# A norm factor by one moving column, a spread in two halves, a fifth filler tile, and the residual update's order pinned anew

## The chip, the cores and the metric

The kernel runs on one core of one Trainium2 chip, as one program. The metric is the time on the device, in microseconds (us), as the median of several executions; the profile is one more execution of the same program, taken by the hardware profiler. A core has five engines with an instruction queue each, worked off in order: TensorE (PE, with its weight loads as PEld), VectorE (DVE), ScalarE (ACT), GpSimd (POOL) and SyncE (SP, which here only issues DMAs). They meet through semaphores: an instruction waits until another engine's count has reached a value.

## The reference, cut to what matters

Two layers over 256 tokens of width 2048. Layer 0 mixes tokens with a state-space mixer, layer 1 with an attention; both layers end in the same tail:

```python
h = x
for i in range(DEPTH):
    hn = rmsnorm(h, norm_mix_pre[i])
    mix = ssd_mixer(hn, ...) if i % 2 == 0 else fox_mixer(hn, ...)
    h = h + rmsnorm(mix, norm_mix_post[i])
    ff = swiglu(rmsnorm(h, norm_ffn_pre[i]), ffn_w_gate[i], ffn_w_up[i], ffn_w_down[i])
    h = h + rmsnorm(ff, norm_ffn_post[i])
    pe = rmsnorm(p[i] @ ple_w_proj[i], ple_norm[i])
    h = h + sigmoid(h @ ple_w_gate[i]) * pe
```

The two lines that add a normed branch to `h` are what the change is about: there are two of them in a layer, four in the program. `rmsnorm(y, w)` multiplies each token's row by one factor, 1/sqrt(mean(y*y) + eps), and each column by `w`.

## The kernel before, in words

**Layout.** Activations lie transposed: 16 chunks of 128 model columns (partitions) by 256 tokens. `h[c]` is chunk c of the residual stream, `m[c]` chunk c of a mixer's or feed-forward's output, `xs[c]` the matmul operand made from `h[c]`.

**Matmuls in two parts.** Every large product is formed from float32 numbers split into a high part and a rest. An operand `xs[c]` holds both (`x[:, 0]` high, `x[:, 1]` low, side by side). A weight stage, 128 x 768 or 128 x 1024 numbers, arrives by DMA as `raw`; ScalarE casts it to the high part `wh` (line 176), VectorE subtracts to get the rest `wl` (line 181). A step of a unit is then, for each output tile, `wh` against both halves of the operand (512 columns, line 238) and `wl` against the high half (256 columns, line 240). `emit_stage` issues the DMA, the cast and the subtraction of the next stage, in that order of the weights, and pins where they stand among the other instructions of ScalarE and VectorE (`issue_after`); four buffers of `wh` and `wl` and six of `raw` rotate. A scheduler makes the queues from this; what is pinned stays so.

**Units.** `unit` works through one block of output columns: it takes the stages one after the other (`next_stage`), calls `pre` for the operands that the next steps need, issues the matmuls of the step, and evacuates the accumulators at the end. The first unit behind each of the four norms has six output tiles and 16 steps, with one stage of 128 x 768 and one operand chunk in each step; it can only run as fast as the operands `xs[c]` are made.

**The norm factor** (`post_norm`, line 399). When the last `m[c]` is squared and summed into `ssb` (128 x 256), `rstd_small` (line 293) multiplies it by a 128 x 128 matrix of ones, for the two halves of the tokens, so that each token's sum stands 128 times in PSUM; one column of each half goes through `ms` (line 300) and GpSimd's power (line 303) to `rs`. `rstd_wide` (line 306) puts `rs` on two diagonals `dg` (line 309), and one matmul of 256 columns with the ones spreads the factors over all partitions (line 312); ScalarE copies them to SBUF as `rwide` (line 313). `rstd_small` and `rstd_wide` are used 18 times in the program; only 4 times by `post_norm`, elsewhere in the midst of a unit.

**Fillers.** TensorE would have nothing to do in that time. Eight tiles of the per-layer product `p @ ple_w_proj` (`filler`, 6 matmuls each, lines 390 to 394) are kept for it: two go ahead of `rstd_small`, two (up to `FILL_B`) between it and the spread, four behind the spread. Each tile's result is copied out of PSUM by ScalarE (line 396, `pp`). One weight stage is emitted ahead of the spread and one behind it (`PRE_A`, `PRE_B`).

**The update** (`mk_update`, line 417). For chunk c: VectorE forms `m[c] * w * rwide` (`scaled`, line 430), adds it to `h[c]` (line 436), ScalarE makes the high part of `xs[c]` (line 269, or 266 in the second norm of a layer, where there is no column factor), VectorE the low part (line 270, or 267). VectorE's steps are chained to each other. Before, the row of them for one chunk was: add of c, `scaled` of c+1, low part of c; the stage's `wl` was pinned ahead of the low part, and its cast behind the high part of the same chunk. For the first two chunks a stage is emitted in the update itself, from then on by `next_stage` in each step.

Of the kernel before, what the change touches and what calls it, by code (L numbers as in the profile page):

```python
# [7 lines left out]
F32 = mybir.dt.float32  # L8
# [6 lines left out]
P = 128  # L15
# [19 lines left out]
FILL_B = 4  # L35
PRE_A = 1
PRE_B = 1
TAIL_STAGES = 2
PACED = 2
WARM = 10  # L40
# [15 lines left out]
def tile_trunk(ctx, tc, a, out):  # L56
# [236 lines left out]
    def rstd_small(acc, n):  # L293
        ps = misc()
        for j in range(2):
            PE.matmul(ps[:, j * P:(j + 1) * P], lhsT=acc[:, j * P:(j + 1) * P], rhs=ones,  # L296
                      start=True, stop=True)
        ms = tmp("ms", (P, 2))
        for j in range(2):
            dmark[0] = V.tensor_scalar(out=ms[:, j:j + 1], in0=ps[:, j * P:j * P + 1], scalar1=1.0 / n,  # L300
                                       scalar2=EPS, op0=mult, op1=add)
        rs = tmp("rs", (P, 2), bufs=3)
        G.tensor_tensor(out=rs, in0=ms, in1=mhalf, op=ALU.pow)  # L303
        return rs

    def rstd_wide(rs, o):
# [5 lines left out]
        PE.matmul(ps[:, :T], lhsT=ones, rhs=dg, start=True, stop=True)  # L312
        A.copy(out=o, in_=ps[:, :T])

# [52 lines left out]
    pts = []  # L367
# [10 lines left out]
    def filler(pp, us):  # L378
        st = [None]

        def tile_(u, t):
# [14 lines left out]
            A.copy(out=pp[4 * u + t], in_=acc[:, :T])  # L396
        return [lambda u=u, t=t: tile_(u, t) for u in us for t in range(4)]

    def post_norm(fill):
# [7 lines left out]
        rstd_wide(rs, rwide)  # L407
        for _ in range(PRE_B):
            emit_stage(mark[0], dmark[0])
        for f in fill[FILL_B:]:  # L410
            f()

# [4 lines left out]
    def mk_update(new, m, wpost, wpre, xs):  # L417
# [10 lines left out]
        def scaled(c):  # L428
            ts[c] = new()
            return V.scalar_tensor_tensor(out=ts[c], in0=m[c], scalar=col(wpost, c), in1=rwide,  # L430
                                          op0=mult, op1=mult)

        def up(c):
            if c == 0:
                chain(lambda: scaled(0))
            chain(lambda: V.tensor_tensor(out=h[c], in0=h[c], in1=ts[c], op=add))
# [41 lines left out]
    def tail(i, mpx, m, pp, mk_next):  # L478
        xs = [newx() for _ in range(NCH)]
        post_norm(filler(pp, (0, 1)))  # L480

        with ExitStack() as st:
# [40 lines left out]
            for half in range(2):  # L523
                acts = [ap_.tile([P, 2, T], F32R, tag="a", name=nm("a")) for _ in range(HALF)]
                c0 = 0
                for n in (GU if half == 0 else GU[::-1]):
                    sgs.clear()
                    up = mk_update(new_sg, m, f"mix_post{i}", f"ffn_pre{i}", xs) if first[0] else None
# [37 lines left out]
        post_norm(filler(pp, (2, 3)))  # L566
# [56 lines left out]
        for u, n in enumerate(OUT0):  # L623
            last = u == len(OUT0) - 1
            up = None
            if u == 0:
                up = mk_update(lambda: pn.tile([P, T], F32, tag="pn", name=nm("pn"), bufs=4), m,
                               f"ffn_post{i}", None, xs2)
# [540 lines left out]
```

## Time and profile before

| | |
|---|---|
| Time before, median of 3 runs | 2781.67 us (2781.13 to 2782.24) |
| The profiled execution's own time | 2781.57 us |
| Its span, first to last instruction | 2779.8 us |
| PE busy | 2758.7 us (99% of the span) |
| DVE busy | 1909.7 us (69%) |
| ACT busy | 1482.3 us (53%) |
| Spread matmuls of the four norms start at | 697.99, 1442.82, 1935.64, 2680.46 us |

Times in rows are counted from the span's start. A row of the timeline gives start, length, engine, line, operation, output<-inputs, shape and count, and in brackets how long the engine had been idle and who ended that. Instructions of one engine overlap a little: the next starts before the last has ended, so the rate is read from the starts. A line of the waits gives who waited for whom, the total, how often, and the longest.

### The profile page before, as it was taken

How to read it: one execution, taken by the hardware profiler on the slowest of the kernel's cores; microseconds unless marked ns; L12 is line 12 of the kernel's file. 1: busy time of each engine (PE TensorE's matmuls, PEld its weight loads, DVE VectorE, ACT ScalarE, POOL GpSimd, SP SyncE). 2: the span in 40 equal slices, each digit the busy share in tenths (PEclk: the TensorE clock that was granted, in tenths of full speed). 3: DMA queues.
4: the chain of work that ended last, by engine and by line, in shares of the span. 5: the costliest groups of instructions: out<-in, count | busy, mean ns of one | idle time of the engine just before them, and what ended most of it. 6: DMA issues, size and time to landing. Idle time of an engine off the chain costs nothing.

```text
span 2779.8 us, 43097 instructions
## 1 busy us (share of the span) xinstructions
PE 2758.7 (99%) x16306; PEld 2446.8 (88%) x16306; DVE 1909.7 (69%) x3165; ACT 1482.3 (53%) x2455; POOL 50.8 (2%) x104
## 2 busy tenths in 40 slices
PE   9999999999999999999999999999999999999999
PEld 8888888889888888888898998888888888888898
DVE  8888888855876645666668656766876545666577
ACT  6586676544654444444446544545554444445454
POOL 0000000000000000000000000000000000000000
PEclk9999999999999999999999999999999999999999
DMA  7666665565666656666556576555666556656554
GB/s 252 198 198 188 190 191 174 156 205 177 184 193 190 191 190 189 189 178 198 193 163 194 168 213 192 178 160 159 195 189 195 191 190 185 193 171 203 196 166 159
DMA packets 262511, 520.08 MB, mean 187 GB/s; under 512 B 17392, under 2 KB 42128, under 8 KB 262304
## 3 DMA queue, kind: packets, MB, share of 16 engines
q1 hardware_dynamic: 258640, 504.96, 59.2%
q0 software_dynamic: 3520, 12.15, 1.5%
q8 instruction: 127, 2.08, 0.3%
q14 instruction: 80, 0.66, 0.1%
q10 hardware_dynamic: 144, 0.24, 0.0%
HBM read 515.10 MB, written 2.18 MB: 186 GB/s over the span
## 4 chain that ended last, share of the span: by engine, by line
PE 97%; DVE 2%; ACT 1%; issue 0%; DMA 0%; POOL 0%; SPq 0%; DVEq 0%; ACTq 0%; POOLq 0%
PE acc L238 56%; PE acc L240 30%; PE acc L234 1%; PE acc L233 1%; PE acc L235 1%; PE acc L228 1%; PE acc L229 1%; PE acc L227 1%; PE mi L820 1%; DVE wl L181 1%; ACT wh L176 0%; PE mi L822 0%; PE mi L312 0%; PE mi L296 0%; PE mi L787 0%
## 5 line engine op out<-in xcount | busy, mean ns | idle before, releaser
L238 PE MATMUL acc<-x,wh 128*128 128x512 f32 x5008 | 1709.3, 393 | 6.1 <-DVE gz L262 1.8
L181 DVE TENSOR_TENSOR wl<-raw,wh 128x1024 fp32r<-128x1024 f32 (+4 forms) x1020 | 1172.1, 1155 | 768.8 <-ACT wh L176 766.9
L176 ACT CAST wh<-raw 128x1024 fp32r<-128x1024 f32 (+4 forms) x1020 | 1007.5, 993 | 1000.4 <-PE acc L238 875.2
L240 PE MATMUL acc<-x,wl 128*128 128x256 f32 x5008 | 1330.0, 282 | 1.8 <-DVE wl L181 1.7
L238 PEld LDWEIGHTS acc<-x,wh 128*128 128x128 f32 x5008 | 925.7, 188 | 192.3 <-issue 4.5
L240 PEld LDWEIGHTS acc<-x,wl 128*128 128x128 f32 x5008 | 930.9, 189 | 28.5 <-DVE wl L181 4.1
L238 PE MATMUL acc<-a,wh 128*128 128x512 f32 x1232 | 425.5, 391 | 0.0
L240 PE MATMUL acc<-a,wl 128*128 128x256 f32 x1232 | 341.9, 282 | 0.0
L238 PEld LDWEIGHTS acc<-a,wh 128*128 128x128 f32 x1232 | 229.9, 188 | 47.1
L240 PEld LDWEIGHTS acc<-a,wl 128*128 128x128 f32 x1232 | 232.6, 189 | 2.2
L238 PE MATMUL acc<-xb,wh 128*128 128x512 f32 x512 | 181.9, 396 | 0.0
L261 ACT COPY tb<-acc 128x256 f32<-128x256 f32 (+1 forms) x401 | 139.5, 369 | 46.4 <-PE acc L240 20.5
L240 PE MATMUL acc<-xb,wl 128*128 128x256 f32 x512 | 145.8, 285 | 0.0
L238 PEld LDWEIGHTS acc<-xb,wh 128*128 128x128 f32 x512 | 95.9, 188 | 19.3
L240 PEld LDWEIGHTS acc<-xb,wl 128*128 128x128 f32 x512 | 96.7, 189 | 0.7 <-issue 0.2
L238 PE MATMUL acc<-xq,wh 128*128 128x512 f32 x224 | 77.6, 390 | 0.0
L802 ACT ACTIVATE E<-ab,bias 128x128 f32<-128x128 f32 x192 | 59.7, 390 | 17.1 <-PE mi L822 16.1
L262 DVE TENSOR_TENSOR g<-acc,tb 128x256 f32<-128x256 f32 x176 | 67.2, 417 | 0.3
L730 DVE SCALAR_TENSOR_TENSOR g<-xr,vec,g 128x256 f32<-128x256 f32 x144 | 62.5, 479 | 4.3 <-ACT g L727 3.9
L240 PE MATMUL acc<-xq,wl 128*128 128x256 f32 x224 | 62.8, 282 | 0.0
L228 PE MATMUL acc<-wl,xb 128*128 128x412 f32 (+1 forms) x160 | 56.8, 355 | 4.0 <-DVE wl L181 4.0
L303 POOL TENSOR_TENSOR rs<-ms,mhalf 128x2 f32<-128x2 f32 x18 | 24.9, 1381 | 1947.5 <-DVE ms L300 1947.5
(207 smaller groups left out, 2185.3 us busy)
## 6 DMA issues: line engine op xcount, KB each, us to landing
raw<-down SPq DMA_DIRECT2D x176, 512.0 KB, 4.0
raw<-ssd_in SPq DMA_DIRECT2D x152, 512.0 KB, 4.5
raw<-gate SPq DMA_DIRECT2D x128, 512.0 KB, 4.4
raw<-up SPq DMA_DIRECT2D x128, 512.0 KB, 4.4
raw<-fox_in SPq DMA_DIRECT2D x64, 512.0 KB, 4.3
raw<-gate SPq DMA_DIRECT2D x64, 384.0 KB, 3.3
raw<-up SPq DMA_DIRECT2D x64, 384.0 KB, 3.6
raw<-ssd_out SPq DMA_DIRECT2D x40, 512.0 KB, 4.1
```

Of the source, the lines that this page charges most:

```text
L176: A.copy(out=wh[:, :kc * n], in_=raw[:, :kc * n])
L181: low[0] = V.tensor_tensor(out=wl[:, :kc * n], in0=raw[:, :kc * n], in1=wh.bitcast(F32)[:, :kc * n], op=sub)
L227: PE.matmul(o, lhsT=xh, rhs=wh[:, c, :], start=st, stop=False)
L228: PE.matmul(o, lhsT=xh, rhs=wl[:, c, :], start=False, stop=False)
L229: PE.matmul(o, lhsT=x[:, 1, t * P:(t + 1) * P], rhs=wh[:, c, :], start=False, stop=sp)
L233: PE.matmul(o, lhsT=w, rhs=x[:, 0, :], start=st, stop=False)
L238: PE.matmul(accs[t], lhsT=wh[:, c, t * P:(t + 1) * P], rhs=x.rearrange("p a n -> p (a n)"), start=st, stop=False)
L240: PE.matmul(accs[t][:, :T], lhsT=wl[:, c, t * P:(t + 1) * P], rhs=x[:, 0, :], start=False, stop=sp)
L261: A.copy(out=tb[:np_], in_=acc[:np_, T:2 * T])
L262: V.tensor_tensor(out=o, in0=acc[:np_, :T], in1=tb[:np_], op=add)
L730: V.scalar_tensor_tensor(out=c, in0=xr[:, k:k + T], scalar=col(f"conv_w{k}", cc), in1=c, op0=mult, op1=add)
L802: A.activation(E[:, i, b * P:(b + 1) * P], ab[:, i, lo:lo + P], AF.Relu, scale=-1.0, bias=bias3[:, b, h0 + i:h0 + i + 1])
```

## The change

The constants: `FILL_B` 4 to 5 (a fifth filler tile between the sums and the spread, three behind it), `PRE_B` gone (no stage behind the spread), `EARLY = 4` in place of `PACED` as the number of chunks that emit a stage in the update, `HELD = 6`: the PSUM copies of filler tiles 6 and 7 are held back until chunk 0's high part.

```diff
     def rstd_small(acc, n):
         ps = misc()
         for j in range(2):
-            PE.matmul(ps[:, j * P:(j + 1) * P], lhsT=acc[:, j * P:(j + 1) * P], rhs=ones,
+            PE.matmul(ps[:, j:j + 1], lhsT=acc[:, j * P:(j + 1) * P], rhs=ones[:, :1],
                       start=True, stop=True)
         ms = tmp("ms", (P, 2))
-        for j in range(2):
-            dmark[0] = V.tensor_scalar(out=ms[:, j:j + 1], in0=ps[:, j * P:j * P + 1], scalar1=1.0 / n,
-                                       scalar2=EPS, op0=mult, op1=add)
+        dmark[0] = V.tensor_scalar(out=ms, in0=ps[:, :2], scalar1=1.0 / n, scalar2=EPS,
+                                   op0=mult, op1=add)
...
         ps = misc()
-        PE.matmul(ps[:, :T], lhsT=ones, rhs=dg, start=True, stop=True)
+        for j in range(2):
+            PE.matmul(ps[:, j * P:(j + 1) * P], lhsT=ones, rhs=dg[:, j * P:(j + 1) * P],
+                      start=True, stop=True)
         A.copy(out=o, in_=ps[:, :T])
+        return ps[:, :T]
...
-        rstd_wide(rs, rwide)
-        for _ in range(PRE_B):
-            emit_stage(mark[0], dmark[0])
+        ps = rstd_wide(rs, rwide)
...
         def scaled(c):
             ts[c] = new()
-            return V.scalar_tensor_tensor(out=ts[c], in0=m[c], scalar=col(wpost, c), in1=rwide,
-                                          op0=mult, op1=mult)
+            return V.scalar_tensor_tensor(out=ts[c], in0=m[c], scalar=col(wpost, c),
+                                          in1=rwide if c else r0, op0=mult, op1=mult)
+
+        def high(c):
+            chain(lambda: V.tensor_tensor(out=h[c], in0=h[c], in1=ts[c], op=add))
+            x = xs[c][:, 0, :]
+            if wpre is None:
+                mark[0] = A.copy(out=x, in_=h[c])
+            else:
+                mark[0] = A.activation(x, h[c], AF.Copy, scale=col(wpre, c))
...
         def up(c):
             if c == 0:
                 chain(lambda: scaled(0))
-            chain(lambda: V.tensor_tensor(out=h[c], in0=h[c], in1=ts[c], op=add))
+                high(0)
+                chain(lambda: scaled(1))
+            hi = mark[0]
+            if c:
+                with tc.issue_after(low[0].ins):
+                    chain(lambda: low_(c))
+            else:
+                for e in held_pp:
+                    with tc.issue_after(hi.ins):
+                        e()
+                held_pp.clear()
+                chain(lambda: low_(c))
             if c + 1 < NCH:
-                chain(lambda: scaled(c + 1))
-            chain(lambda: split(h[c], xs[c], None if wpre is None else col(wpre, c)))
+                if c:
+                    chain(lambda: scaled(c + 1))
+                high(c + 1)
             turn.append(prev[0])
             turn_a[0] = mark[0]
-            if c < PACED and len(emitted) <= taken[0] + 3:
-                emit_stage(mark[0], prev[0])
+            if c < EARLY and len(emitted) <= taken[0] + 3:
+                emit_stage(hi, prev[0])
```

`low_` is the old `split`'s second half under a name of its own. `up(c)` now reaches one chunk further than before: it ends with the add and the high part of chunk c+1, and it is these that `turn` and `turn_a` hand to the next `emit_stage`.

What this does to VectorE's queue at the first norm (layer 0), from the sums to chunk 1. The names carry buffer numbers: `h_83` is `h[0]`, `h_84` `h[1]` and so on, `x_7668` is `xs[0]`, `x_7669` `xs[1]`; `sg` is the output of `scaled`, `mi` a PSUM tile. Before:

```order
L300 TENSOR_SCALAR ms_7703<-mi_7700 128x1 x2
L181 TENSOR_TENSOR wl_7711<-raw_7708,wh_7710 128x768
L309 TENSOR_SCALAR dg_7730<-cst,rs_7706 128x128 x2
L181 TENSOR_TENSOR wl_7739<-raw_7736,wh_7738 128x768
L430 SCALAR_TENSOR_TENSOR sg_7805<-m_0_6583,vec,rwide 128x256
L436 TENSOR_TENSOR h_83<-h_83,sg_7805 128x256
L430 SCALAR_TENSOR_TENSOR sg_7808<-m_1_6584,vec,rwide 128x256
L270 SCALAR_TENSOR_TENSOR x_7668<-h_83,vec,x_7668 128x256
```

The same piece of VectorE's queue after the change, with the semaphores that each waits for:

```order
L300 TENSOR_SCALAR ms_7703<-mi_7700 128x2 [waits PE_49]
L182 TENSOR_TENSOR wl_7710<-raw_7707,wh_7709 128x768 [waits DMAHW4_49,Activation_49]
L309 TENSOR_SCALAR dg_7737<-cst,rs_7705 128x128 [waits Pool_49]
L309 TENSOR_SCALAR dg_7737<-cst,rs_7705 128x128
L436 SCALAR_TENSOR_TENSOR sg_7797<-m_0_6583,vec,mi_7740 128x256 [waits Activation_49]
L440 TENSOR_TENSOR h_83<-h_83,sg_7797 128x256 [waits DVE_49]
L436 SCALAR_TENSOR_TENSOR sg_7801<-m_1_6584,vec,rwide 128x256
L451 SCALAR_TENSOR_TENSOR x_7668<-h_83,vec,x_7668 128x256 [waits Activation_49]
```

The second `wl` has gone from ahead of the first update, and the first update reads the spread's PSUM tile `mi_7740`; it waits for ScalarE's count alone (`Activation_49`), not for TensorE's (`PE_49`).

Now the same first unit five chunks on, where every chunk's round looks alike. VectorE before, from the low part of chunk 4 to that of chunk 6:

```order
L270 SCALAR_TENSOR_TENSOR x_7672<-h_87,vec,x_7672 128x256
L436 TENSOR_TENSOR h_88<-h_88,sg_7870 128x256
L430 SCALAR_TENSOR_TENSOR sg_7893<-m_6_6589,vec,rwide 128x256
L181 TENSOR_TENSOR wl_7889<-raw_7886,wh_7888 128x768
L270 SCALAR_TENSOR_TENSOR x_7673<-h_88,vec,x_7673 128x256
L436 TENSOR_TENSOR h_89<-h_89,sg_7893 128x256
L430 SCALAR_TENSOR_TENSOR sg_7916<-m_7_6590,vec,rwide 128x256
L181 TENSOR_TENSOR wl_7912<-raw_7909,wh_7911 128x768
L270 SCALAR_TENSOR_TENSOR x_7674<-h_89,vec,x_7674 128x256
```

and ScalarE before, in the same rounds:

```order
L269 ACTIVATE x_7672<-h_87,vec 128x256
L176 CAST wh_7888<-raw_7886 128x768
L269 ACTIVATE x_7673<-h_88,vec 128x256
L176 CAST wh_7911<-raw_7909 128x768
L269 ACTIVATE x_7674<-h_89,vec 128x256
```

After, VectorE:

```order
L451 SCALAR_TENSOR_TENSOR x_7672<-h_87,vec,x_7672 128x256
L436 SCALAR_TENSOR_TENSOR sg_7872<-m_5_6588,vec,rwide 128x256
L440 TENSOR_TENSOR h_88<-h_88,sg_7872 128x256
L182 TENSOR_TENSOR wl_7891<-raw_7888,wh_7890 128x768
L451 SCALAR_TENSOR_TENSOR x_7673<-h_88,vec,x_7673 128x256
L436 SCALAR_TENSOR_TENSOR sg_7895<-m_6_6589,vec,rwide 128x256
L440 TENSOR_TENSOR h_89<-h_89,sg_7895 128x256
L182 TENSOR_TENSOR wl_7914<-raw_7911,wh_7913 128x768
L451 SCALAR_TENSOR_TENSOR x_7674<-h_89,vec,x_7674 128x256
```

and ScalarE:

```order
L445 ACTIVATE x_7672<-h_87,vec 128x256
L279 ACTIVATE sq_8249<-h_87 128x256
L445 ACTIVATE x_7673<-h_88,vec 128x256
L177 CAST wh_7890<-raw_7888 128x768
L445 ACTIVATE x_7674<-h_89,vec 128x256
L177 CAST wh_7913<-raw_7911 128x768
```

Before, the `wl` ahead of chunk 5's low part (`x_7673`) was that of `wh_7888`, whose cast stands behind chunk 4's high part (`x_7672`): one round back. After, it is that of `wh_7890`, whose cast stands behind the high part of chunk 5 itself. For the four stages of the first chunks (`EARLY`) the cast still stands one round back; from chunk 5 to chunk 15 all eleven are as shown, and the same holds at each of the four norms.

More of the change, by code (lines that the diff above doesn't have):

```diff
@@ L365, in noop @@
         pass
-    pts = []
+    pts, held_pp = [], []
     def load_p(i, mp):
@@ L395, in tile_ @@
                           start=False, stop=c == 1)
-            A.copy(out=pp[4 * u + t], in_=acc[:, :T])
+            e = lambda: A.copy(out=pp[4 * u + t], in_=acc[:, :T])
+            if 4 * (u - us[0]) + t < HELD:
+                e()
+            else:
+                held_pp.append(e)
         return [lambda u=u, t=t: tile_(u, t) for u in us for t in range(4)]
```

24 lines of the change are left out of this document (17 added, 7 removed).

## The prediction

> **What bounds the kernel now.** I read the page first, and there the engines' busy times:
>
> ```profile
> PE 2758.7 (99%) x16306; PEld 2446.8 (88%) x16306; DVE 1909.7 (69%) x3165; ACT 1482.3 (53%) x2455; POOL 50.8 (2%) x104
> ```
>
> TensorE bounds the kernel as a whole, and there are only some 20 us in which it does nothing. Whatever the change saves must come out of those, or out of TensorE's own work; whatever makes TensorE wait is paid in full. Among the waits of TensorE one line is this change's place:
>
> ```profile
> PE mi L312 <- DVE dg L309: 3.5, 4, 0.9
> ```
>
> Four times 0.9 us in front of the spread (L312), once for each norm. So I read the timeline at the first norm, TensorE, VectorE and ScalarE apart:
>
> ```profile
> 695.12 0.60 PE L296 MATMUL mi<-ones,ssb 128*128 128x128 f32 x4
> 697.99 0.70 PE L312 MATMUL mi<-dg,ones 128*128 128x256 f32 x2 [0.86 <-DVE dg L309]
> 701.47 0.50 PE L238 MATMUL acc<-x,wh 128*128 128x512 f32 x1
> ...
> 695.76 0.22 DVE L300 TENSOR_SCALAR ms<-mi 128x1 f32<-128x1 f32 x2 [0.64 <-PE mi L296]
> 697.46 0.48 DVE L309 TENSOR_SCALAR dg<-cst,rs 128x128 f32<-128x128 f32 x2 [0.61 <-POOL rs L303]
> 699.13 0.48 DVE L430 SCALAR_TENSOR_TENSOR sg<-m,vec,rwide 128x256 f32<-128x256 f32 x1 [0.33 <-ACT rwide L313]
> 699.65 0.43 DVE L436 TENSOR_TENSOR h<-h,sg 128x256 f32<-128x256 f32 x1
> 700.93 0.48 DVE L270 SCALAR_TENSOR_TENSOR x<-h,vec,x 128x256 fp32r<-128x256 f32 x1 [0.46 <-ACT x L269]
> ...
> 698.73 0.37 ACT L313 COPY rwide<-mi 128x256 f32<-128x256 f32 x1 [1.18 <-PE mi L312]
> 700.38 0.52 ACT L269 ACTIVATE x<-h,vec 128x256 fp32r<-128x256 f32 x1
> ```
>
> One chain runs through all three engines: sums 695.12, `ms`, power, `dg`, spread 697.99, copy 698.73, update 699.13, add, high part 700.38, low part 700.93, first matmul of the unit 701.47. It is 6.35 us long, and fillers cover all but about 1.2.
>
> Then comes what the chain leads into, the unit's 16 steps. Chunk rounds in the third norm (VectorE, ScalarE), and TensorE's starts of its steps 1 and 15:
>
> ```profile
> 1952.37 0.42 DVE L436 TENSOR_TENSOR h<-h,sg 128x256 f32<-128x256 f32 x1
> 1952.70 0.48 DVE L430 SCALAR_TENSOR_TENSOR sg<-m,vec,rwide 128x256 f32<-128x256 f32 x1
> 1953.10 0.95 DVE L181 TENSOR_TENSOR wl<-raw,wh 128x768 fp32r<-128x768 f32 x1
> 1953.96 0.48 DVE L270 SCALAR_TENSOR_TENSOR x<-h,vec,x 128x256 fp32r<-128x256 f32 x1
> 1954.36 0.42 DVE L436 TENSOR_TENSOR h<-h,sg 128x256 f32<-128x256 f32 x1
> ...
> 1952.82 0.51 ACT L269 ACTIVATE x<-h,vec 128x256 fp32r<-128x256 f32 x1 [0.76 <-DVE h L436]
> 1953.23 0.82 ACT L176 CAST wh<-raw 128x768 fp32r<-128x768 f32 x1
> ...
> 1941.32 0.39 PE L238 MATMUL acc<-x,wh 128*128 128x512 f32 x1
> 1970.44 0.39 PE L238 MATMUL acc<-x,wh 128*128 128x512 f32 x1
> ```
>
> TensorE's step is (1970.44 - 1941.32)/14 = 2.08 us. VectorE's round, add to add, is 1.99 us and never idle: it keeps 0.09 ahead per step. The `wl` that starts at 1953.10 cannot be that of the cast that starts at 1953.23: it uses the round before's. That lag lets ScalarE's cast run beside VectorE. This loop, not the norm's chain, is what the new order changes most.
>
> **The change, part by part.**
>
> *The chain in front.* Sums over one moving column: four passes, 0.11 us apart today ((0.60 - 0.28)/3). Nothing in the trace has one column; nearest are small float32 passes of 64 (two views by line first, for the lengths of passes):
>
> ```profile
> L296 PE MATMUL mi<-ones,ssb x32: 270/275/377, 32.9 to 2677.9; 128*128 128x128 f32 x32
> ...
> L312 PE MATMUL mi<-dg,ones x36: 377/378/483, 39.1 to 2738.8; 128*128 128x256 f32 x36
> ...
> 80.18 0.22 PE L699 MATMUL mi<-cst,dtT 64*128 64x64 f32 x1
> 80.24 0.22 PE L701 MATMUL mi<-cst,adT 64*128 64x64 f32 x1
> ```
>
> The last two start 0.06 apart. I take 0.06, bounds 0.02 and 0.11 (as now); the last pass starts 0.15 earlier and is 0.05 shorter (0.22 for 0.275). One `ms` instead of two: -0.07. So `dg` begins 0.27 earlier. The spread's first half needs the first `dg` alone, 0.20 before the second: spread at 697.52, its last pass 0.10 shorter (0.275 for 0.378), copy at 698.16, update at 698.56, 0.57 earlier than now. The high part today waits 0.30 behind a filler's copy (add ends 700.08, 700.38 begins); with tiles 6 and 7 held it follows at once. First matmul 0.86 earlier, at 700.61. TensorE's cover: the fifth tile brings 0.70 (6 matmuls of 256 columns, at a sixth of the loop's 2.08 for 768), so it reaches the spread at about 697.5 without the 0.86 idle, but has only three tiles behind it and then waits about 0.6 for the operand. Gain 0.86 at each norm, bounds 0.4 (one-column passes no faster, held copies worth nothing) and 1.2 (all that is idle).
>
> *First update from PSUM.* In the built program it waits for ScalarE's count, and the only ScalarE work it can need there is the copy of the same PSUM tile to `rwide`. So it starts when it could have read `rwide`: I count 0. Without that wait it would start up to 0.40 earlier (698.73 to 699.13), 1.6 us over the four. The Trainium skill's page "PSUM — Partial Sum Buffer", section "PSUM bank collisions raise a hardware error", has the reason: two engines must not access one bank at the same time, two readers included, so they are put in order by semaphores. By that rule the gain is none, as the order has it; no run here shows the wait yet.
>
> *The loop.* The order rows: from chunk 5 to chunk 15 the `wl` ahead of a chunk's low part belongs to a cast that stands behind that same chunk's high part. One round is now a single chain through both engines: add ends, high part, cast, `wl`, low part, next `scaled`, next add. For the second norm of a layer the links are different instructions; cast to `wl` has its row too:
>
> ```profile
> 1968.48 0.84 ACT L176 CAST wh<-raw 128x768 fp32r<-128x768 f32 x1 [0.46 <-ACT wh L176]
> 1969.36 0.96 DVE L181 TENSOR_TENSOR wl<-raw,wh 128x768 fp32r<-128x768 f32 x1 [0.34 <-ACT wh L176]
> 1447.60 0.42 DVE L267 TENSOR_TENSOR x<-h,x 128x256 fp32r<-128x256 f32 x1
> 1447.93 0.42 DVE L436 TENSOR_TENSOR h<-h,pn 128x256 f32<-128x256 f32 x1
> 1451.56 0.41 ACT L266 CAST x<-h 128x256 fp32r<-128x256 f32 x1
> 1451.87 0.83 ACT L176 CAST wh<-raw 128x768 fp32r<-128x768 f32 x1
> ```
>
> First norm of a layer: add 0.42, to the high part 0.03 (1952.79 to 1952.82), high part to cast 0.41, cast 0.82, to `wl` 0.04, `wl` to low part 0.86, low part to `scaled` 0.40, `scaled` to the add that needs it 0.52 (699.13 to 699.65; today `scaled` stands further ahead and the add does not wait for it). Sum 3.50 us. Second norm: 0.42 + 0.03 + 0.31 + 0.83 + 0.04 + 0.86 + 0.33 + 0.52 = 3.34. TensorE needs 2.08 and has nothing else to do: it loses 1.42 or 1.26 in each of eleven steps, 15.6 or 13.9 us. Before chunk 5 the casts stand a round back and VectorE's round is 0.40 + 0.52 + 0.33 + 0.86 = 2.11, or 2.04: no loss, and at chunk 4 a slack of 0.1 or 0.4 (1.97 + 3 x 2.11 = 8.3, or 1.87 + 3 x 2.04 = 8.0, from chunk 0's low part, against 4 x 2.08 + 0.1 for the start). Left: 15.5 and 13.5.
>
> *Behind the loop* three more `wl` of the next unit stand in VectorE's queue, then the evacuation that TensorE waits for. Today VectorE is ahead and the third `wl` waits for TensorE:
>
> ```profile
> 732.78 0.39 PE L238 MATMUL acc<-x,wh 128*128 128x512 f32 x1
> 733.78 0.96 DVE L181 TENSOR_TENSOR wl<-raw,wh 128x768 fp32r<-128x768 f32 x1 [1.12 <-ACT wh L176]
> 1477.45 0.39 PE L238 MATMUL acc<-x,wh 128*128 128x512 f32 x1
> 1478.66 1.23 DVE L181 TENSOR_TENSOR wl<-raw,wh 128x1024 fp32r<-128x1024 f32 x1 [0.85 <-ACT wh L176]
> 1479.80 0.42 DVE L279 TENSOR_TENSOR ssp<-ssp,sq 128x256 f32<-128x256 f32 x1
> ```
>
> It starts 1.00 and 1.21 us behind TensorE's step 15. After, the last low part begins its own length and 0.06 before that step, 0.54 (0.48), and the third `wl` follows 0.40 + 2 x 0.86 (0.33 + 2 x 1.14) later: at 1.58 and 2.13. Cost 0.6 and 0.9.
>
> *Elsewhere.* Fourteen more sums stand among matmuls of busy units, where a pass saved is time saved: 14 x 4 x 0.05 = 2.8 us less. The spread's four passes stream the same 512 columns as its two; I count 0.01 for the two more, 0.2 in all. Net -2.6, bounds 0 and -5 (0.02 per pass). The scheduler has also shuffled instructions in the state-space mixer; TensorE hardly waits there today, I count 0, give or take 2. The stages and their DMAs keep their order on SP and are asked for later, never earlier.
>
> **The sum.** First norms: -0.86 + 15.5 + 0.6 = +15.2, twice. Second norms: -0.86 + 13.5 + 0.9 = +13.5, twice. With -2.6: +54.8. On the profiled execution's 2781.57 that is 2836.4; the median of the runs shown is 0.1 higher, so 2836.5, 2.0% slower.
>
> **The rivals.**
>
> *The loop keeps up* (chance 0.10, not slower). The mechanism is the lag: it decides whether the cast behind which a round's `wl` waits ended before that round's add. If VectorE does find it done, a round is 2.11 or 2.04 us. Today's rows run just so, with 0.13 us between `wl` and a cast it doesn't need. But the dependent add and the `wl` that moved into the loop (0.86) use up VectorE's lead. From the update at 698.56 it reaches chunk 0's low part in 1.5, chunk 3's in 1.97 + 2 x 2.11 more, chunk 15's in 12 x 2.11 and the third `wl` behind the loop in 0.40 + 2 x 0.86: at 733.7, as today (733.78). So the first norms give their 0.86 back there; the second, at 2.04, keep about 0.65. Time: 2 x -0.65 - 2.6 = -3.9, 2777.8, faster by less than a measurement can tell. Against it stands the order itself: the high part reads the add's output, the cast queues behind it, and `wl` reads the cast. It would take an engine that runs its queue out of order.
>
> *Half clock* (0.07). TensorE would do 2.08 us of work in 3.50: 59%. The clock by windows, in front of the two longest waits of the second layer's start:
>
> ```profile
> 1537.70:1541.00 3.30, 1.81 (x12) 1.00 0.25 50
> 1541.10:1544.40 3.30, 3.24 (x18) 1.00 0.68 242
> 1544.50:1547.80 3.30, 0.97 (x5) 1.00 0.06 3
> 1547.90:1551.20 3.30, 3.30 (x11) 0.50 0.72 180
> ```
>
> After 0.97 us of work in 3.30 the next stretch ran at half clock; after 1.81 (55%) it did not. The loop's 59% is on the good side, near the row that stayed at full clock. If it fell all the same, a step takes 4.16 us: 11 x 0.66 x 2 + 11 x 0.82 x 2 = 32.6 more, 2869; with every second stretch, 2853. The Trainium skill speaks for this rival: "TensorE: Matmul & The Clock Gate", section "A second HAM failure mode: psum-queue depth-cycling", says that short idle times between groups of matmuls, each too short to matter alone, can make the gate swing between half and full clock. This trace so far leans against it, by its one row at 55%.
>
> *The PSUM read pays* (inside the range): 1.6 us less, 2835.
>
> **How the numbers follow.** The serial loop at full clock is likeliest, 0.83: 2836.5. Its unknowns: 0.1 us in a round is 4.4 us over 44 rounds; sums and shuffle 3 either way; so 2828 to 2846. Up to 2853 the half-clock case is let in by half; the case that keeps up is left out. Range 2828 to 2853. About 0.2% (5.6 us) is what a measurement can tell from no change: the serial loop and the half clock are slower, 0.90; of the other 0.10 most lies within (2777.8), 0.08; 0.02 is for faster by more, if the norms also gain all of their idle 1.2.
>
> **What would show it.** Right: idle time on TensorE in front of L238 in the 34 us behind each norm, put down to VectorE's low part, about 13 to 16 us a norm; steps of 2.1 up to chunk 4 and 3.3 to 3.5 from chunk 5; in each round add, high part, cast, `wl`, low part end to end; spread at its matmul without a wait; first update at the end of the copy. Wrong: rounds of 2.1 with a `wl` ahead of its neighbour cast's end; a granted clock of 0.5 in these stretches; or a first matmul no earlier behind the sums than 6.3 us.

## The result: 2.2% slower, and the profile after

| | before | after |
|---|---|---|
| median of the runs | 2781.71 us (2781.13 to 2782.24, 4 runs) | 2842.43 us (2841.39 to 2843.46, 4 runs) |
| ratio, 95% interval | | 1.0217 (1.0205 to 1.0229) |
| profiled execution: time, span | 2781.57, 2779.8 us | 2841.39, 2839.6 us |

The time is slower by 60.7 us; 54.8 were forecast, and 2842.43 lies inside the range of 2828 to 2853.

The page of the changed kernel, its engines (most line numbers are one or more higher than before: 239 is the matmul of the step, 182 `wl`, 177 the cast, 451 and 450 the low parts, 440 the add):

```profile
PE 2768.8 (98%) x16342; PEld 2446.2 (86%) x16342; DVE 1917.8 (68%) x3147; ACT 1483.4 (52%) x2455; POOL 47.7 (2%) x104
```

The three engines do about as much as before; nothing in this line shows 60 us. The view of waits does (who waits, for what: us in total, times, longest):

```profile
PE acc L239 <- DVE x L451: 24.8, 22, 1.3
PE acc L239 <- DVE x L450: 22.8, 24, 1.0
...
PE acc L239 <- ACT wh L177: 3.7, 4, 1.2
PE acc L239 <- DVE gz L263: 3.3, 2, 1.7
PE acc L239 <- DVE sg L263: 1.7, 2, 0.9
```

The wait for the spread (4 times 0.9) is no longer among the waits. In its place TensorE waits 46 times for a low part (lines 451 and 450), about 1 us each. One round of the loop behind the first norm, VectorE, ScalarE, and the first matmul of two steps:

```profile
721.30 0.42 DVE L440 TENSOR_TENSOR h<-h,sg 128x256 f32<-128x256 f32 x1
723.03 0.96 DVE L182 TENSOR_TENSOR wl<-raw,wh 128x768 fp32r<-128x768 f32 x1 [1.31 <-ACT wh L177]
723.90 0.48 DVE L451 SCALAR_TENSOR_TENSOR x<-h,vec,x 128x256 fp32r<-128x256 f32 x1
724.30 0.48 DVE L436 SCALAR_TENSOR_TENSOR sg<-m,vec,rwide 128x256 f32<-128x256 f32 x1
724.81 0.43 DVE L440 TENSOR_TENSOR h<-h,sg 128x256 f32<-128x256 f32 x1
...
721.75 0.51 ACT L445 ACTIVATE x<-h,vec 128x256 fp32r<-128x256 f32 x1 [2.27 <-DVE h L440]
722.17 0.82 ACT L177 CAST wh<-raw 128x768 fp32r<-128x768 f32 x1
...
721.01 0.47 PE L239 MATMUL acc<-x,wh 128*128 128x512 f32 x1 [1.19 <-DVE x L451]
724.53 0.47 PE L239 MATMUL acc<-x,wh 128*128 128x512 f32 x1 [1.20 <-DVE x L451]
```

Read the starts in order of time: add 721.30, high part 721.75, cast 722.17, `wl` 723.03, low part 723.90, scaled product 724.30, next add 724.81. Each starts where the one before it ends, on two engines by turns, and each engine idles while the other works (VectorE 1.31, ScalarE 2.27 per round). The round is 3.51 us, and TensorE's step has become 3.52 (721.01 to 724.53). Its clock stayed whole (columns: the stretch, its length, then busy us with counts of PE, PEld, DVE, ACT and POOL, then the granted clock, the DMA share, GB/s):

```profile
713.00:723.00 10.00, 6.64 (x35) 5.48 (x36) 6.01 (x12) 3.71 (x6) 0.00 (x0) 1.00 0.42 116
723.00:733.00 10.00, 6.42 (x34) 4.99 (x34) 6.53 (x12) 3.17 (x6) 0.00 (x0) 1.00 0.39 95
```

The chain in front of the same norm, TensorE, VectorE, ScalarE:

```profile
696.29 0.50 PE L297 MATMUL mi<-ones,ssb 128*128 128x1 f32 x4
...
698.86 0.68 PE L313 MATMUL mi<-dg,ones 128*128 128x128 f32 x4
...
702.04 0.51 PE L239 MATMUL acc<-x,wh 128*128 128x512 f32 x1 [0.44 <-DVE x L451]
...
696.83 0.16 DVE L300 TENSOR_SCALAR ms<-mi 128x2 f32<-128x2 f32 x1 [0.54 <-PE mi L297]
...
698.48 0.49 DVE L309 TENSOR_SCALAR dg<-cst,rs 128x128 f32<-128x128 f32 x2 [0.61 <-POOL rs L303]
699.98 0.48 DVE L436 SCALAR_TENSOR_TENSOR sg<-m,vec,mi 128x256 f32<-128x256 f32 x1 [1.01 <-ACT rwide L315]
...
699.57 0.37 ACT L315 COPY rwide<-mi 128x256 f32<-128x256 f32 x1
...
700.95 0.51 ACT L445 ACTIVATE x<-h,vec 128x256 fp32r<-128x256 f32 x1 [0.31 <-DVE h L440]
```

From the sums' start to the first matmul of the unit it is 5.75 us (6.35 before). The spread is reached without a wait; the first update starts at 699.98, right at the end of the copy (699.57 + 0.37).

**Where the 59.8 us of the profiled execution are.** I took four starts at each norm from TensorE's timelines: first filler, first matmul of the unit, its step 15, first matmul of the next unit (before / after):

| norm | first filler | unit | step 15 | next unit |
|---|---|---|---|---|
| 1 | 693.74 / 694.92 | 701.47 / 702.04 | 732.78 / 749.12 | 735.46 / 752.31 |
| 2 | 1438.28 / 1455.09 | 1446.13 / 1462.34 | 1477.45 / 1507.42 | 1480.61 / 1511.41 |
| 3 | 1931.39 / 1961.80 | 1939.12 / 1968.85 | 1970.44 / 2015.93 | 1973.12 / 2019.11 |
| 4 | 2675.92 / 2721.89 | 2683.83 / 2729.14 | 2715.12 / 2774.22 | 2718.29 / 2778.20 |

How much the lag (after less before) grows from column to column gives each part: in the heads (first filler to unit) -0.61, -0.60, -0.68, -0.66; in the loops (unit to step 15) +15.77, +13.76, +15.76, +13.79; behind them +0.51, +0.83, +0.50, +0.81; in front of the first norm +1.18, and in all the stretches between and behind the norms -0.54 together. The sum is 59.8.

| part | forecast | measured |
|---|---|---|
| four heads | -3.4 | -2.6 |
| four loops | +58.0 | +59.1 |
| behind the loops | +3.0 | +2.7 |
| elsewhere | -2.6 | +0.6 |

### The profile page after: what moved, and what is told of

It is laid out like the page before. It is cut to its first block, busy times and chain, and to the rows that moved or that the text cites. A ratio compares the mean times of both kernels' runs of the same rounds, so it can differ in the third digit from the quotient of the medians.

```text
span 2839.6 us, 43195 instructions
## 1 busy us (share of the span) xinstructions
PE 2768.8 (98%) x16342; PEld 2446.2 (86%) x16342; DVE 1917.8 (68%) x3147; ACT 1483.4 (52%) x2455; POOL 47.7 (2%) x104
## 4 chain that ended last, share of the span: by engine, by line
PE 91%; DVE 6%; ACT 2%; issue 1%; DMA 0%; SPq 0%; ACTq 0%; DVEq 0%
PE acc L239 53%; PE acc L241 28%; DVE wl L182 3%; ACT wh L177 2%; PE acc L236 1%; PE acc L234 1%; PE acc L235 1%; PE acc L229 1%; PE acc L230 1%; PE acc L228 1%; DVE h L440 1%; PE mi L853 1%; DVE pn L436 0%; DVE sg L436 0%; DVE x L451 0%
## 5 line engine op out<-in xcount | busy, mean ns | idle before, releaser
L280 DVE TENSOR_TENSOR ssb<-ssb,sq 128x256 f32<-128x256 f32 x120 | 50.4, 420 | 12.6 <-ACT sq L279 8.6
```

The source lines that it names most:

```text
L280: last_v[0] = V.tensor_tensor(out=acc, in0=acc, in1=sq, op=add)
```

## Experiments

The theory: the loss is one serial chain, because the cast that a round's `wl` needs stands behind that same round's high part. Rival A: the add that now stands right behind its own scaled product slows VectorE. Rival B: a weight stage less is asked for ahead of the unit, and weights come late. The kernel before ran in each of the sets below, at medians of 2781.43, 2781.49 and 2781.68 us.

**The cast one round back.** One line of the changed kernel:

```diff
-            turn_a[0] = mark[0]
+            turn_a[0] = hi
```

> The change, with the weight cast pinned behind the high part of the chunk before instead of the chunk's own. Theory (one serial chain through ScalarE and VectorE, because the cast stands behind its own chunk's high part): the cast runs beside VectorE again, a round falls from 3.51 and 3.36 us to VectorE's own 2.1, TensorE's steps from chunk 5 on are 2.08 to 2.12, the heads keep their 0.6 each; of the 59.1 us lost in the four loops all but about 1 comes back and the 2.7 behind them too: 2779 to 2782 us. Rival A (the add that now stands right behind its own scaled product is what slows VectorE): that order is untouched here, so rounds stay near 3.4 and the time at 2835 to 2842. Rival B (a weight stage less is asked for ahead of the unit, so stages come late): untouched too, 2835 to 2842.

Measured: 2783.84 us (11 runs), ratio to before 1.0010 (1.0001 to 1.0019). 58.6 of the 60.7 us are gone with one line, and both rivals, whose orders were left as they were, are out. VectorE and ScalarE in this kernel:

```profile
721.87 0.43 DVE L440 TENSOR_TENSOR h<-h,sg 128x256 f32<-128x256 f32 x1
722.21 0.95 DVE L182 TENSOR_TENSOR wl<-raw,wh 128x768 fp32r<-128x768 f32 x1
...
723.99 0.43 DVE L440 TENSOR_TENSOR h<-h,sg 128x256 f32<-128x256 f32 x1
...
722.74 0.82 ACT L177 CAST wh<-raw 128x768 fp32r<-128x768 f32 x1
```

The `wl` at 722.21 starts ahead of the cast beside it (722.74) and without a wait: it uses the cast before. VectorE's round is 2.12 us (721.87 to 723.99) and never idle. But that is 0.04 more than TensorE's step, and the time is 1.8 us over the top of what was expected: the loops of the first norms still lose 0.4 each (steps of 2.10 to 2.14), and 0.63 to 0.66 stay lost behind each of the four. There three `wl` of the next unit stand ahead of the evacuation that TensorE waits for:

```profile
734.20 2.70 DVE L182 TENSOR_TENSOR wl<-raw,wh 128x768 fp32r<-128x768 f32 x3
...
737.62 0.51 PE L239 MATMUL acc<-x,wh 128*128 128x512 f32 x1 [1.04 <-DVE sg L263]
```

VectorE reaches them too late to do them in TensorE's shadow; it takes them in one go.

**Only the add made independent.** The scaled product one round ahead of its add, the cast left where the change has it:

```diff
             if c + 1 < NCH:
-                if c:
-                    chain(lambda: scaled(c + 1))
                 high(c + 1)
+                if c + 2 < NCH:
+                    chain(lambda: scaled(c + 2))
```

> The change, with each scaled product issued one round earlier, so that no add stands right behind the product that it needs; the cast stays behind its own chunk's high part. Theory (serial chain through the cast): only the link from the scaled product to the add, 0.51 us, leaves the round: 3.00 and 2.85 us, a loss of 11 x 0.92 and 11 x 0.77 per norm instead of 15.8 and 13.8, in all 37 instead of 59: about 2819 us (2815 to 2823). Rival A (the dependent add): rounds of 2.1, 2779 to 2784 us. Rival B (late stages): no change, 2838 to 2842.

Measured: 2817.74 us (4 runs), ratio 1.0129 (1.0115 to 1.0142). TensorE's steps are 2.99 and 2.84 us, against 3.00 and 2.85 worked out: the link of 0.51 left the chain, and the chain stayed. The dependent add is a link worth 24.7 us of the loss, not its cause: with it left in and the cast one round back only some 2 us were lost.

**Only the new update order.** The kernel before with the new `mk_update`, but four filler tiles, both stages ahead, old sums and spread, and `rwide` read by every update:

```diff
-    def mk_update(new, m, wpost, wpre, xs):
+    def mk_update(new, m, wpost, wpre, xs):   # body of the change, without r0 and held copies
```

> The kernel before with only the new update order (no one-column sums, no split spread, four filler tiles, both stages asked for ahead, rwide read by every update). Theory: the order alone carries the loss. With a stage more ahead the serial chain begins at chunk 6, so ten rounds of 3.51 and 3.36: 2 x 10 x 1.43 + 2 x 10 x 1.28 = 54 us, less up to 1 per norm for the greater lead, plus 0.5 to 0.8 behind each loop: 2833 to 2840 us. Rival B (the stage that is no longer asked for ahead of the unit makes the weights late): with the stage back the loss is gone, 2780 to 2785.

Measured: 2836.67 us (4 runs), ratio 1.0198 (1.0184 to 1.0212). The steps are 3.51 and 3.36 from chunk 6 on, a chunk later than in the change, as the stage more ahead lets them. Rival B is out once more: that stage takes one of eleven slow rounds away and leaves the others.

**Every cast in the loop twice.** The change, with a doubled link:

```diff
-            A.copy(out=wh[:, :kc * n], in_=raw[:, :kc * n])
+            for _ in range(twice):      # 2 inside the update loops, else 1
+                A.copy(out=wh[:, :kc * n], in_=raw[:, :kc * n])
```

> The change with each weight cast inside the four update loops made twice (the second writes the same numbers again; so does it for the first few casts behind a loop). Theory (the cast is a link of the serial chain): each of the 11 slow rounds is longer by a whole cast behind another, 0.74 us: 4.25 and 4.10 us, 4 x 11 x 0.74 = 33 us more, plus up to 2 behind each loop: 2873 to 2884 us. Rival A (the dependent add is the bound, the cast runs beside it): 2842 to 2850. On the half-clock rival: TensorE is busy 2.08 of 4.25 us, 49%, less than the 59% of the change; if its clock falls at all in this loop the granted clock of the loop shows 0.5 here, which would hide in the round (4.16 of 4.25).

Measured: 2889.15 us (2 runs), ratio 1.0386 (1.0367 to 1.0405), above the 2873 to 2884 expected. The mechanism is as expected, the price of the second cast was too low: rounds are 4.37 and 4.22 us, 0.86 longer, not 0.74, since the second cast, into the same tile, waits for ScalarE's own count and so for the end of the first; and the last round is longer by more (5.71 and 5.98), as its `wl` starts only at the end of the fourth of six casts in a row: those of the next unit's stages are doubled too. ScalarE, and the windows of this kernel:

```profile
724.52 1.68 ACT L180 CAST wh<-raw 128x768 fp32r<-128x768 f32 x2
```

```profile
713.00:723.00 10.00, 6.96 (x24) 5.41 (x24) 5.49 (x10) 4.21 (x7) 0.00 (x0) 0.66 0.28 79
723.00:733.00 10.00, 5.65 (x30) 4.51 (x30) 5.38 (x11) 4.28 (x7) 0.00 (x0) 1.00 0.34 84
733.00:743.00 10.00, 8.47 (x33) 6.64 (x31) 4.35 (x8) 5.35 (x9) 0.00 (x0) 0.66 0.39 113
```

Two casts take 1.68, twice 0.82 and 0.04. And here the granted clock falls to 0.66 in two of three windows: TensorE has 2.08 us of work in 4.37, 48%. In the change it had 59%, and the clock stayed at 1.00. The rounds are no longer for it: 2.08 us of work are 4.16 at half clock. But at the second norm the clock stays at 0.50 from 1525.0 to 1538.7 us, 9 us past the start of step 15 (1529.7), and from that step to the next norm's first filler it takes 3.0 us longer than in the change (behind the first and third norm 0.5 and 1.1, behind the fourth nothing). What part the doubled casts have in this was not tried apart.

**Only the norm factor.** The kernel before with the new `rstd_small` and `rstd_wide`, nothing else changed:

```diff
-            PE.matmul(ps[:, j * P:(j + 1) * P], lhsT=acc[:, j * P:(j + 1) * P], rhs=ones,
+            PE.matmul(ps[:, j:j + 1], lhsT=acc[:, j * P:(j + 1) * P], rhs=ones[:, :1],
...
-        PE.matmul(ps[:, :T], lhsT=ones, rhs=dg, start=True, stop=True)
+        for j in range(2):
+            PE.matmul(ps[:, j * P:(j + 1) * P], lhsT=ones, rhs=dg[:, j * P:(j + 1) * P],
+                      start=True, stop=True)
```

> The kernel before with only the norm factor's part (sums with one moving column, one scaling of the mean, spread in two halves). From the changed kernel's rows: four one-column passes take 0.36 us as four of 128 columns do. Theory: nothing is saved among the busy units; each of the four heads is 0.15 to 0.35 earlier: 0.6 to 1.4 us less; and the instructions of the state-space mixer, which the scheduler moves, cost between 0 and 1.2: 2780 to 2782.5. Rival (the prediction's own term: a pass of one column saves 0.05, 2.8 us over the fourteen sums outside the norms): 2777 to 2779.

Measured: 2781.15 us (11 runs), ratio 0.9999 (0.9990 to 1.0008): no difference that can be measured, where the prediction's term alone would give 2.8 us. In the profile the heads are 0.35 to 0.69 shorter, and 1.20 us are lost in front of the first norm.

**A half as wide stationary tile.** What does a pass of a sum cost? The kernel with the cast one round back, each sum over 128 tokens made as two over 64:

```diff
-            PE.matmul(ps[:, j:j + 1], lhsT=acc[:, j * P:(j + 1) * P], rhs=ones[:, :1],
-                      start=True, stop=True)
+            for q in (0, 64):
+                PE.matmul(ps[q:q + 64, j:j + 1], lhsT=acc[:, j * P + q:j * P + q + 64],
+                          rhs=ones[:, :1], start=True, stop=True)
```

> The change with the cast of the chunk before, and each sum over 128 tokens with one moving column made as two of 64 tokens (stationary tile 128 x 64, one moving column): eight passes instead of four for each sum. If the time of a pass with one column is that of its stationary tile's columns: 0.06 a pass, 0.45 us for a sum, as long as now, and 2783 to 2786 us. If every pass costs a fixed 0.11 us whatever its shape: 0.8 to 0.9 us for a sum, and 18 x 0.45 = 8 us more, 2790 to 2793.

Measured: 2781.69 us in one execution, below the 2783 to 2786 expected; a single execution decides nothing here, the rows do. TensorE around one sum that stands among a unit's matmuls, in the kernel before, in one with one moving column (that with the halves at the norms alone, below), and with half tiles:

```profile
217.87 0.39 PE L238 MATMUL acc<-x,wh 128*128 128x512 f32 x1
218.10 0.61 PE L296 MATMUL mi<-ones,gss 128*128 128x128 f32 x4
218.46 0.71 PE L238 MATMUL acc<-x,wh 128*128 128x512 f32 x2
```

```profile
217.91 0.39 PE L239 MATMUL acc<-x,wh 128*128 128x512 f32 x1
218.14 0.50 PE L297 MATMUL mi<-ones,gss 128*128 128x1 f32 x4
218.50 0.71 PE L239 MATMUL acc<-x,wh 128*128 128x512 f32 x2
```

```profile
217.97 0.39 PE L239 MATMUL acc<-x,wh 128*128 128x512 f32 x1
218.29 0.40 PE L298 MATMUL mi<-ones,gss 128*64 128x1 f32 x8
218.62 0.38 PE L241 MATMUL acc<-x,wl 128*128 128x256 f32 x1
```

From the matmul ahead to the one behind it is 0.59, 0.59 and 0.65 us; the first two kernels agree within 0.01 at each of the program's eighteen sums. Less the 0.23 of the matmul ahead, the sum takes 0.36 with 128 equal columns, 0.36 with one, and 0.42 with eight passes of half the stationary tile. Read one by one, these eight start in four pairs: 0.007 us from pass to pass within a pair, 0.08, 0.06 and 0.06 from pair to pair. So from the first of them to the last it is 0.20; the other 0.22 of the 0.42 stand ahead of the first pass (0.32 behind the matmul ahead instead of 0.23) and behind the last (0.13). At a fixed 0.11 for every pass it would have been about 0.9. The loads of the stationary tile show what paces them; four of them in the changed kernel, and one by itself:

```profile
212.61 0.53 PEld L297 LDWEIGHTS mi<-ones,gss 128*128 128x128 f32 x4
213.06 0.19 PEld L239 LDWEIGHTS acc<-x,wh 128*128 128x128 f32 x1
```

Four loads in 0.53 us, the last of them 0.19 long, are 0.11 apart: the passes follow at the pace of the loads. So a pass of one column lasts as long as its stationary tile needs, not its moving columns. The Trainium skill has the price of the load on the page "TensorE: Matmul & The Clock Gate", section "LDWEIGHTS (loading the stationary operand)": the tile's number of columns divided by 1.2, in ns; by estimate from that, 0.107 us for 128 columns and 0.053 for 64. The 0.11 between passes agrees with the first, and the 0.06 between pairs is near the second, though it is two loads at a time that keep this pace; the load's own row is longer, 0.19.

**VectorE's loop order of before, the rest of the change kept.** In `up` (the low part is no longer pinned behind a `wl`):

```diff
                 chain(lambda: scaled(0))
                 high(0)
-                chain(lambda: scaled(1))
             hi = mark[0]
...
             if c + 1 < NCH:
-                if c:
-                    chain(lambda: scaled(c + 1))
-                high(c + 1)
+                chain(lambda: scaled(c + 1))
+            chain(lambda: low_(c))
             turn.append(prev[0])
-            turn_a[0] = mark[0]
+            turn_a[0] = hi
...
+            if c + 1 < NCH:
+                high(c + 1)
```

> The change with VectorE's loop order of the kernel before (scaled product one round ahead of its add, cast one round back); new norm factor, fifth filler tile, held copies and the first update from PSUM kept. Theory: VectorE's round is about 2.0 us against TensorE's 2.08, so it gains lead in the loop, and the three weight parts behind the loop are no longer late: the 0.4 per first norm and the 0.65 behind each loop that the kernel with the cast alone put back still lost are gone (2 x 0.4 + 4 x 0.65 = 3.4 us). Heads 0.6 earlier, 1.2 to 1.7 later in front of the first norm: 2779 to 2781.5 us. Rival (the 0.65 behind the loop comes from the stage that is no longer asked for ahead of the unit, not from VectorE's lead): 2781.5 to 2783.5.

Measured: 2780.25 us (11 runs), ratio 0.9995 (0.9986 to 1.0004). All steps are as in the kernel before (2.08 us from the second on), nothing is lost behind the loops, and the third `wl` there waits again, VectorE being ahead:

```profile
734.47 0.96 DVE L182 TENSOR_TENSOR wl<-raw,wh 128x768 fp32r<-128x768 f32 x1 [0.94 <-ACT wh L177]
...
736.16 0.50 PE L239 MATMUL acc<-x,wh 128*128 128x512 f32 x1 [0.44 <-DVE sg L263]
```

That VectorE's lead, not the stage ahead of the unit, is what hides these `wl` is shown with it: this kernel, too, has one stage less.

**The copy behind the first update.** The kernel just told, and ScalarE reads the spread's PSUM tile only when VectorE has:

```diff
-        ps = rstd_wide(rs, rwide)
+        ps = rstd_wide(rs, None)          # no copy there
...
                 chain(lambda: scaled(0))
+                with tc.issue_after(prev[0].ins):
+                    A.copy(out=rwide, in_=r0)
```

> The same as the kernel with the loop order of before, and ScalarE's copy of the spread to rwide pinned behind the first update, so that the update need not wait for the other reader of its PSUM tile. Theory (the first update waits only for that copy, so reading PSUM brought nothing in the change): the update starts 0.40 earlier, and the first matmul with it, as far as TensorE is idle there: 0.4 in the first norm of a layer, 0.2 in the second, 1.2 us in all below the kernel with the loop order of before. Rival (an update that reads PSUM takes longer, or rwide comes too late for the second update): no gain or a loss, the first matmul no earlier.

Measured: 2779.01 us (11 runs), ratio 0.9992 (0.9983 to 1.0001); 1.24 below the kernel without it. At the first norm (TensorE, VectorE, ScalarE):

```profile
699.00 0.68 PE L313 MATMUL mi<-dg,ones 128*128 128x128 f32 x4
...
701.86 0.50 PE L239 MATMUL acc<-x,wh 128*128 128x512 f32 x1
...
699.71 0.48 DVE L437 SCALAR_TENSOR_TENSOR sg<-m,vec,mi 128x256 f32<-128x256 f32 x1 [0.61 <-PE mi L313]
...
700.23 0.37 ACT L459 COPY rwide<-mi 128x256 f32<-128x256 f32 x1 [0.66 <-DVE sg L437]
```

The update starts 0.03 behind the spread's end (699.68) instead of 0.44, and takes 0.48 from PSUM as from SBUF. At all four norms the first matmul is 0.32 or 0.33 earlier behind the first filler (0.4 and 0.2 by turns had been expected). So reading PSUM pays 0.3 us a norm if the other reader of the tile is put behind it; as the change has it, it cannot. The 1.24 us are less than the two intervals; that all four heads are shorter by the same is what carries them.

**Which part of the norm factor pays, and what it costs elsewhere.** Three kernels on that base: the spread in halves only at the four norms; in one piece everywhere; and that with the old sums (128 equal columns, two `ms`).

```diff
-        for j in range(2):
-            PE.matmul(ps[:, j * P:(j + 1) * P], lhsT=ones, rhs=dg[:, j * P:(j + 1) * P],
-                      start=True, stop=True)
+        w = P if o is None else T          # halves only where a norm asks for them
+        for j in range(0, T, w):
+            PE.matmul(ps[:, j:j + w], lhsT=ones, rhs=dg[:, j:j + w], start=True, stop=True)
```

> The kernel with the copy behind the first update, and the spread in two halves only at the four norms; the other spreads in one piece, which leaves TensorE's order in the state-space mixer that of the kernel before but for 17 rows. Theory (the 1.1 us that the changed kernel loses in front of the first norm come from the scheduler's other order there, which the two halves elsewhere bring about): the waits at 144 and 145 us are gone, the first filler stands 0 to 0.3 later than before instead of 1.2 (up to 1 more if the start-up is slow in the profiled execution), and the time is 1.1 below the 2779.0 of that kernel: 2777.5 to 2778.3 us. Rival (it is start-up or chance, not order): 2778.7 to 2779.3.

> As the kernel with the split at the norms alone, but with all spreads in one piece, the norms' too; sums with one moving column. The spread needs both halves of dg and its copy comes 0.2 to 0.3 later at each norm: 0.8 to 1.2 us more than with the split at the norms: 2778.3 to 2779.5 us.

> As the kernel with all spreads in one piece, and the sums again over 128 equal moving columns with two scalings of the mean; TensorE's order is otherwise the same to 16 rows. Theory (a pass lasts as long as its stationary tile's 128 columns, one moving column or 128): the sums outside the norms cost the same, and only the four heads are 0.1 to 0.15 later: 0.4 to 0.6 us more than with one column: 2779 to 2780. The prediction's term (0.05 saved in each of 4 passes in 14 sums): 2.8 more and the heads: 2781.5 to 2783.

Measured (11 runs each): 2777.84, ratio 0.9987 (0.9978 to 0.9996); 2778.56, 0.9988 (0.9979 to 0.9997); 2779.18, 0.9991 (0.9982 to 1.0000). The steps between these medians are smaller than the intervals; the traces carry them. From first filler to unit the four heads are 6.79, 6.93, 6.80, 6.92 us in the first, 6.98, 7.11, 6.99, 7.11 in the second, 7.13, 7.26, 7.14, 7.27 in the third: the halves are worth 0.18 or 0.19 at a norm, the one column with one `ms` 0.15 or 0.16. Four times that is 0.7 and 0.6, what the medians show. For 2.8 us from the other sums there is no room.

And the 1.18 us in front of the first norm: the halves elsewhere let the scheduler take another order in the state-space mixer. TensorE and ScalarE of the change, then ScalarE of the kernel before:

```profile
144.13 1.19 PE L239 MATMUL acc<-x,wh 128*128 128x512 f32 x4 [0.46 <-ACT wh L177]
...
140.49 1.48 ACT L840 ACTIVATE E<-E 128x1536 f32<-128x1536 f32 x1
141.87 1.27 ACT L835 ACTIVATE E<-ab,bias 128x128 f32<-128x128 f32 x4
143.03 1.99 ACT L177 CAST wh<-raw 128x1024 fp32r<-128x1024 f32 x2
```

```profile
141.82 1.05 ACT L176 CAST wh<-raw 128x1024 fp32r<-128x1024 f32 x1
...
143.65 1.04 ACT L176 CAST wh<-raw 128x1024 fp32r<-128x1024 f32 x1
144.59 1.50 ACT L807 ACTIVATE E<-E 128x1536 f32<-128x1536 f32 x1
```

The cast stands behind the 1.48 us of L840 instead of ahead of it, and TensorE waits. With the halves at the norms alone that wait is gone, and the first filler is 0.24 us later than before instead of 1.18. By the sum at 258 us the change is 0.85 behind the kernel before (258.35 against 257.50), the kernel with the halves at the norms alone 0.00, while near 33 us all three are within 0.1; so the loss does not stem from the start of the program. What the rest of that 0.85 is, beyond the wait of 0.46, was not tried apart; the 0.33 behind it come later, where the other kernel loses its 0.24. That kernel is the fastest of all: 3.8 us under the one before, with an interval that lies below 1, and 64.6 us under the change.

## Why the prediction was right, point by point

- **The loop** (15.5 and 13.5 per norm): right in mechanism and size. Steps of 3.51 and 3.36 stand where 3.50 and 3.34 were summed from the rows of before, from chunk 5 on as the order rows said. Putting back the lag of one cast took the loss away; lengthening the cast lengthened the round by the same 0.86; taking the add's link out shortened it by that link. The size was short by 1.1 in all, mostly 0.01 to 0.02 per round. One sign came out smaller than said: TensorE's waits for a low part are 12.4 and 11.4 us a norm by the view of waits, not 13 to 16, though the loops lost 15.8 and 13.8. A wait is counted from the modelled end of the last matmul (0.28 long, where in a full stream the next one starts 0.12 behind its start), so the view shows 1.20 of the 1.43 lost in a round.
- **Behind the loop** (0.6 and 0.9): 0.51 and 0.82. That it belongs to VectorE's lead is shown by the kernel with the cast alone put back (0.65 left) against the one with the whole order of before (0).
- **The head** (0.86 earlier): 0.60 to 0.68. The mis-sized step is "four passes" at 0.06: one column does not shorten a pass, so `dg` came 0.15 earlier, not 0.27; and the halves gave 0.18, not 0.30, as the spread's four passes take 0.68 where its two took 0.70, and stand behind the fifth filler tile. The held copies gave their 0.28. TensorE idled 0.44 ahead of the unit, about 0.6 had been said.
- **Elsewhere** (-2.6, bounds 0 and -5): +0.6, outside these bounds. Two errors. The price of 0.06 was read from passes that differ from a sum's in more than their few moving columns: they are transposes, their stationary tile has 64 rows (64*128 in their row), and their load takes 0.14 us, not 0.19. With the sums' own tile one moving column saved nothing; which of those differences made the 0.06 was not tried. And the scheduler's new order in the mixer, put at 0 give or take 2, costs 1.1. These 3.2 us and the head's 0.9 are most of what the forecast was short.
- **First update from PSUM, counted 0**: right. It starts at the end of the copy. The rule of the Trainium skill's page "PSUM — Partial Sum Buffer", section "PSUM bank collisions raise a hardware error", that two readers of a bank are put in order, is what the profile shows; the run with the order turned round gained 1.24 us, against the 1.6 given as the bound.
- **The rivals.** That the loop keeps up is out by the steps. Half clock is out for the change (1.00 at 59%), though perhaps not by much: at 48% it came, in stretches. The Trainium skill ("TensorE: Matmul & The Clock Gate", section "A second HAM failure mode: psum-queue depth-cycling") tells of short idle times between groups of matmuls that make the clock swing. Here they did not at 59 to 70% busy, and did at 48 to 49%. There the swing cost nothing within a round, since 4.16 us at half clock fit into 4.2 to 4.4, but up to 3.0 us went where it reached past the loop.

## What to carry to other kernels

Where two engines feed each other once per round, look from which round the operand comes: one round of lag lets them work side by side (2.1 us), no lag adds them up (3.5), and no busy time in the profile tells the difference. Take the price of a small matmul from a row of the same kind with the same stationary tile. And when an edit outside the place under study moves the scheduler, limit it to that place: here the halves paid 0.7 us at four norms and cost 1.1 elsewhere.

## What the runs showed of the hardware

- A float32 pass with a 128 x 128 stationary tile is 0.11 us behind the one before it whether 128 or one column moves. With 128 x 64 tiles for the two halves of the output's partitions, passes start in pairs 0.007 us apart, the later pairs 0.06 apart, and the whole sum is no cheaper (0.42 against 0.36).
- TensorE's clock stayed at 1.00 through the loop with 59% of work in each round of 3.5 us, and with 48% in each of 4.4 it swung between 0.50 and 1.00 (0.66 over 10 us in two of three windows).
- A cast into the tile of the cast before it starts 0.86 us behind it, though two casts into different tiles are 0.74 apart (in the kernel before, at the first norm, a row of two takes 1.56, one takes 0.82).
- The first 12 us differ by up to 1.9 us between profiled executions of kernels with the same order there (first sum at 32.8 to 33.1 us, but 34.65 in the kernel with the new update order alone and 34.79 in the one with the old sums). In these two TensorE starts 11 and 12 matmuls between 7.4 and 10.6 us, before the change 20; in the first of them the granted clock is 0.50 there. Differences of that size in front of the first norm say nothing without a row that shows where they arise.
